# Weights' second part by an accumulating DMA instead of a VectorE subtraction, in a two-layer hybrid inference step

## Chip, core and metric

One core of one Trainium2 chip runs the whole program. The metric is the device time of one execution in microseconds, as the median of several executions.

## What is computed

Two layers of a hybrid backbone, for 512 latent and 128 context tokens of width 2048, in float32. The reference, cut to its trunk:

```python
for l in range(DEPTH):
    hp = _rmsnorm(xp, norm_g[l]) * (1.0 + sc_p) + sh_p
    hs = _rmsnorm(xs, norm_g[l]) * (1.0 + sc_s) + sh_s
    if l % 2 == 0:      # attention and Hyena, one projection in, one out
        out_p, (k_ctx, v_ctx) = _even_mixer(hp, *ev)
        out_s, _ = _even_mixer(hs, *ev, ctx_k=cache_k[:, j], ctx_v=cache_v[:, j])
    else:               # RG-LRU behind a short convolution, times a gate
        out_p, st = _odd_mixer(hp, *od)
        out_s, _ = _odd_mixer(hs, *od, h0=jnp.moveaxis(state_lru[:, j], 1, 0))
    xp = xp + g_p * out_p
    xs = xs + g_s * out_s
```

Each mixer projects all 640 tokens with a large weight matrix (`h @ w_in`, `mixed @ w_out`). The scale, shift and gate vectors come from a second large product, `silu(c) @ mod_w`.

## The kernel before

**The projections.** TensorE multiplies in a rounded float32 (`F32R`), so that each factor is split in two: `wh` is the weight rounded, `wl` what the rounding left, and likewise `h` and `l` for the activations (`mh`, `ml` or `md` for the mixers' outputs). Each product is three matmuls, `wh*h`, `wh*l` and `wl*h`. Weights come in 241 half chunks of 128 x 8 x 128 elements (512 KB). `project` (L810) walks a chunk's two halves over 16 tiles of activations and two column blocks of 320 tokens: 48 matmuls for each half chunk.

**The weight stream.** Class `Stream` (L453) holds three buffers each of `raw`, `wh` and `wl`. `load` (L466) issues the DMA of a half chunk from SyncE's queue. `advance` (L474) rounds it on ScalarE (`wh`) and hands the rest to `finish` (L494), which subtracts on VectorE and then issues the load that takes this half chunk's place in `raw`:

```python
(self.G if self.pooled and i % 2 else self.V).tensor_sub(wl, raw, wh.bitcast(F32))
self.load(i + 1 + RAWS)
```

`pooled` is never set, so all subtractions are VectorE's. `keep_ahead` (L513) splits up to two half chunks ahead of the one that TensorE is using.

**The stages.** A start stage (normalisation, Hyena filters, the first gates; 19 half chunks are split there), attention over eight query chunks q0 to q7 (`attend` L1746, `queries` L1846), Hyena in four blocks of long convolutions (`long_conv` L1958), the first output projection (`out_project` L2224, which also writes `x1d` and scales the tiles `xo` for layer 1), the RG-LRU (`scans` L2367) and the second output projection. In every stage the projections' matmuls (tile `acc`) fill TensorE between the mixers' own work.

**Side sums.** `side_mods` (L661) makes 16 groups of the second product on the side: `mod_w` tiles come by SyncE (`mraw`), ScalarE multiplies (`mprod`) and GpSimd adds up (`macc`), or VectorE does both in one instruction where it is free (from Hyena to the first output projection). A group ends with two small steps on TensorE (`m<-macc,ones`, then `m<-ident,mprod`). The last four tiles of layer 1's input wait for groups 11 and 12 of these.

**The order.** The program is a list of coroutines that a planner (`Order`, `Clock`) runs ahead of time with costs of its own; what it emits is a fixed order on each engine and queue. So a change in one cost or one instruction moves others. An engine runs its order strictly; one that waits holds back everything behind it. The same goes for SyncE, which issues all loads and stores (weights, `mraw`, `ga<-gad` gates, `mixd` and `x1d` stores).

Of the kernel before, what the change touches and what calls it, by code (L numbers as in the profile page):

```python
# [10 lines left out]
F32 = mybir.dt.float32  # L11
F32R = mybir.dt.float32r
AF = mybir.ActivationFunctionType
ALU = mybir.AluOpType
# [160 lines left out]
class Clock:  # L175
# [17 lines left out]
    def __init__(self):  # L193
        self.t = {"PE": 0.0, "V": 0.0, "S": 0.0, "G": 0.0, "Q": 0.0, "DMA": 0.0}
        self.table, self.last = None, 0.0
        self.writes, self.reads, self.start = {}, {}, {}
        self.held = {"V": [], "G": []}
# [255 lines left out]
class Stream:  # L453


    def __init__(self, engines, clock, pool, ahead=2):
        self.V, self.S, self.G, self.Q = engines
        self.pooled = False
        self.clock, self.pool, self.ahead = clock, pool, ahead
        self.src, self.raw, self.parts, self.left = [], {}, {}, {}  # L460
        self.loaded = self.split = self.taken = 0
# [32 lines left out]
    def finish(self, i):  # L494

        if i not in self.left:
            return
        raw, (wh, wl) = self.left.pop(i), self.parts[i]
        (self.G if self.pooled and i % 2 else self.V).tensor_sub(wl, raw, wh.bitcast(F32))
        self.load(i + 1 + RAWS)  # L500

    def take(self, od):
# [20 lines left out]
@with_exitstack  # L523
def tile_kernel(ctx: ExitStack, tc: tile.TileContext, A: dict, O: dict):
    with tc.manual_schedule():
        _kernel(ctx, tc, A, O)


def _kernel(ctx, tc, A, O):
# [6 lines left out]
    def pool_of(stack, name, bufs=1, **kw):  # L536
        return Pool(stack.enter_context(tc.tile_pool(name=name, bufs=bufs, **kw)), clock, bufs)
# [10 lines left out]
    ws = Stream((V, S, G, Q), clock, wpool)  # L548
# [112 lines left out]
    def side_mods(groups, raws, accs, prods, ring):  # L661
        todo = [(l, g, k) for l, g in groups for k in range(16)]
        raw, n = {}, 0
        for j, (l, g, k) in enumerate(todo):
# [17 lines left out]
            for v in range(2):  # L682
                c, a = csil[:, k, v:v + 1], acc[v]
                while True:
                    if clock.t["V"] + IDLE[0] <= od.time and not left[v] and clock.ready([a], [a], "V") <= od.time:
                        if k == 0:
# [933 lines left out]
            V.tensor_scalar(fr[:, :, i, :], yv[:, :, i, :], sc, None, op0=ALU.mult)  # L1620

    IDLE = [99]
    mods = ctx.enter_context(ExitStack())
    mp = pool_of(mods, "mods", bufs=1)
    r_raw = Ring(mp, [128, 512], F32, "mraw", 2)
# [261 lines left out]
    first_out = []  # L1887
    IDLE[0] = 0.5
    with ExitStack() as st:
# [332 lines left out]


    def out_project(op, layer, src, parts, first, keep, finish, xout, sqa, last=None):  # L2224

        r_x = Ring(op, [128, T], F32, "xr", 3 if last else 2)
# [9 lines left out]
        def out(i, x, o):  # L2236
# [10 lines left out]
            def then():  # L2247
                r_x.free(x)
                if keep is not None:
                    Q.dma_start(out=keep[i], in_=o[:, 0:T])  # L2250
                if i == 0:
                    S.activation(sqa, o[:, 0:T], AF.Square)
                else:
                    while not r_sq.ready():
                        yield 0.3
                    sq = r_sq.get()
                    S.activation(sq, o[:, 0:T], AF.Square)
                    yield
                    V.tensor_add(sqa, sqa, sq)
                    r_sq.free(sq)  # L2260
                yield
                yield from finish(i, o)
                yield
                xout[i] = o
# [20 lines left out]
    first_lru = []  # L2285
    IDLE[0] = 0.3
    with ExitStack() as st:
# [38 lines left out]
    parts2, first_out, mixed_done = [None] * 16, [], {}  # L2326
    IDLE[0] = 99
    with ExitStack() as st:
# [447 lines left out]
```

## Time and profile before

| | |
|---|---|
| median of three runs | 2297.33 us (2296.53 to 2302.62) |
| the profiled execution | 2299.91 us, its span 2298.1 us |
| TensorE (PE) busy | 2130.1 us, 93% |
| VectorE (DVE) busy | 1673.0 us, 73% |
| ScalarE (ACT) busy | 1086.3 us, 47% |
| GpSimd (POOL) busy | 845.3 us, 37% |
| DMA | 320.62 MB, 16 engines busy 41.5% |

How to read the rows below. Nearly all instructions are recorded at one line, L318, a helper; they are told apart by tiles, output before the arrow. PE is the matmul, PEld the weight load beside it, SPq SyncE's queue. A window's row gives for PE, PEld, DVE, ACT and POOL the busy time with the number of instructions, then the granted clock of TensorE as a share of full speed, the busy share of the DMA engines and GB/s. A row of waits is: who waited, for whom, us in total, times, the longest. A timeline row is: start, duration, engine, operation, and in brackets the idle time before and what ended it. A row of a group ends with busy time, mean ns of one, and after the bar the engine's idle time before them and what ended most of it. A row of DMA issues ends with KB each and the median us from issue to landing. Matmuls are pipelined, so one lasts 310 ns while the next starts 147 ns after it.

### The profile page before, as it was taken

The numbers are of one execution on the slowest core, as the hardware profiler recorded it, in microseconds if no ns is written. First come the engines' busy times: TensorE is split into PE (matmuls) and PEld (weight loads), VectorE is DVE, ScalarE is ACT, GpSimd is POOL, SyncE is SP. The second block draws the span as 40 slices with busy tenths as digits, with TensorE's granted clock in tenths as the row PEclk, the third lists the DMA queues.
The fourth block names the chain that finished last, engine by engine and source line by source line (L and its number), as shares of the span: only waits on it lengthen the run. The fifth ranks groups of instructions, "written<-read, shape, count | busy, mean of one in ns | idle before, by whom it ended". The sixth has DMA issues, their size and how long they took to land. (4 is left out here: it accounts for less than half of the span.)

```text
span 2298.1 us, 37534 instructions
## 1 busy us (share of the span) xinstructions
PE 2130.1 (93%) x14567; PEld 2025.0 (88%) x14567; DVE 1673.0 (73%) x2560; ACT 1086.3 (47%) x1814; POOL 845.3 (37%) x678
## 2 busy tenths in 40 slices
PE   4899989988989999999998999899999999999997
PEld 1579888877878999999987999799999999999997
DVE  6968775898877888887887676787886667783334
ACT  5555555555553333333353333576565554662222
POOL 3424443445344666566563222444530101110002
PEclk9899999999999999999998999999999999999998
DMA  9864434222225444444455555333322222243223
GB/s 367 301 247 131 136 114 135 84 100 86 93 95 194 140 147 147 140 139 146 148 200 175 191 188 183 98 116 114 117 79 88 85 85 86 80 171 109 97 97 131
DMA packets 127449, 320.62 MB, mean 140 GB/s; under 512 B 14246, under 2 KB 22279, under 8 KB 127272
## 3 DMA queue, kind: packets, MB, share of 16 engines
q1 hardware_dynamic: 125480, 313.20, 40.5%
q0 software_dynamic: 1792, 5.04, 0.7%
q8 instruction: 114, 1.87, 0.3%
q14 instruction: 63, 0.52, 0.1%
HBM read 281.86 MB, written 36.32 MB: 138 GB/s over the span
## 5 line engine op out<-in xcount | busy, mean ns | idle before, releaser
L318 PE MATMUL acc<-h,wh 128*128 128x320 f32 x2544 | 810.0, 318 | 24.9 <-DVE xo L318 9.0
L318 PE MATMUL acc<-h,wl 128*128 128x320 f32 x2544 | 793.0, 312 | 0.0
L318 PE MATMUL acc<-l,wh 128*128 128x320 f32 x2544 | 792.4, 311 | 0.0
L318 POOL TENSOR_TENSOR macc<-macc,mprod 128x512 f32<-128x512 f32 x289 | 434.7, 1504 | 559.2 <-ACT mprod L318 474.1
L318 PEld LDWEIGHTS acc<-h,wh 128*128 128x128 f32 x2544 | 485.2, 191 | 36.0 <-DVE xo L318 9.3
L318 PEld LDWEIGHTS acc<-l,wh 128*128 128x128 f32 x2544 | 484.7, 191 | 0.1
L318 PEld LDWEIGHTS acc<-h,wl 128*128 128x128 f32 x2544 | 483.6, 190 | 0.0
L318 ACT CAST wh<-raw 128x1024 fp32r<-128x1024 f32 x241 | 252.4, 1047 | 413.0 <-PE acc L318 370.0
L318 DVE TENSOR_TENSOR wl<-raw,wh 128x1024 fp32r<-128x1024 f32 x241 | 318.0, 1320 | 171.5 <-ACT wh L318 169.2
L318 PE MATMUL acc<-mh,wh 128*128 128x320 f32 (+2 forms) x1024 | 318.9, 311 | 11.2 <-ACT mh L318 8.8
L318 ACT ACTIVATE mprod<-mraw,vec 128x512 f32<-128x512 f32 x289 | 209.1, 724 | 237.6 <-POOL macc L318 169.5
L318 PE MATMUL acc<-mh,wl 128*128 128x320 f32 (+2 forms) x1024 | 318.3, 311 | 0.0
L318 PE MATMUL acc<-ml,wh 128*128 128x320 f32 (+2 forms) x928 | 288.0, 310 | 2.4 <-DVE ml L318 2.4
L318 DVE SCALAR_TENSOR_TENSOR macc<-mraw,vec,macc 128x512 f32<-128x512 f32 x191 | 186.2, 991 | 100.8 <-DMA mraw<-in_mod_w_dram 77.3
L318 PEld LDWEIGHTS acc<-mh,wh 128*128 128x128 f32 x1024 | 193.2, 189 | 14.6 <-ACT mh L318 9.2
L318 PEld LDWEIGHTS acc<-mh,wl 128*128 128x128 f32 x1024 | 193.6, 189 | 0.0
L318 PEld LDWEIGHTS acc<-ml,wh 128*128 128x128 f32 x928 | 175.1, 189 | 4.1 <-DVE ml L318 3.7
L318 POOL COPY stout<-hs 128x1 f32<-128x1 f32 x32 | 20.5, 639 | 319.2 <-DVE hs L318 319.2
L318 PE MATMUL g<-xhl,wh 128*128 128x322 f32 x512 | 115.7, 314 | 2.2 <-ACT ri L318 2.2
L318 POOL TENSOR_TENSOR y<-y,t 128x256 f32<-128x256 f32 x80 | 84.2, 1072 | 43.0 <-DVE t L318 34.1
L318 POOL TENSOR_TENSOR xo<-xo,sq 128x384 f32<-128x384 f32 (+1 forms) x13 | 11.5, 916 | 239.8 <-ACT sq L318 239.8
L318 DVE SCALAR_TENSOR_TENSOR xo<-acc,modc,xr 128x128 f32<-128x128 f32 (+3 forms) x96 | 38.8, 434 | 82.6 <-PE acc L318 73.7
(303 smaller groups left out, 3369.4 us busy)
## 6 DMA issues: line engine op xcount, KB each, us to landing
mraw<-in_mod_w_dram SPq DMA_DIRECT2D x256, 256.0 KB, 3.3
raw<-in_w_in_dram SPq DMA_DIRECT2D x95, 512.0 KB, 4.0
mraw<-in_mod_w_dram SPq DMA_DIRECT2D x64, 512.0 KB, 7.4
raw<-in_c_in_dram SPq DMA_DIRECT2D x64, 512.0 KB, 3.7
raw<-in_c_out_dram SPq DMA_DIRECT2D x34, 512.0 KB, 3.9
raw<-in_w_out_dram SPq DMA_DIRECT2D x32, 512.0 KB, 4.0
hd<-ef SPq DMA_DIRECT2D x48, 256.0 KB, 3.9
raw<-in_c_gates_dram SPq DMA_DIRECT2D x16, 512.0 KB, 3.5
```

The costliest lines, as they stand in the source:

```text
L318: f(*args, **kw)
```

## The change

From attention on, ScalarE writes the negated `wh` into `wl`, and GpSimd issues a DMA that adds `raw` onto it. VectorE no longer takes part. The start stage keeps the subtraction.

```diff
@@ class Stream, __init__
-        self.pooled = False
+        self.adding = False
@@ class Stream, finish
         raw, (wh, wl) = self.left.pop(i), self.parts[i]
-        (self.G if self.pooled and i % 2 else self.V).tensor_sub(wl, raw, wh.bitcast(F32))
+        if self.adding:
+            self.S.activation(wl, wh.bitcast(F32), AF.Identity, scale=-1.0)
+            self.G.dma_start(out=wl, in_=raw, accum_op=ALU.add)
+        else:
+            self.V.tensor_sub(wl, raw, wh.bitcast(F32))
         self.load(i + 1 + RAWS)
@@ _kernel, after the start stage
     IDLE = [99]
+    ws.adding = True
     mods = ctx.enter_context(ExitStack())
```

Of the 241 half chunks 222 are changed: VectorE has 222 subtractions less, ScalarE 222 negations more, GpSimd 222 DMA issues more. The planner also shares the side sums out anew: 310 instead of 289 products on ScalarE with as many adds on GpSimd, 180 instead of 196 steps on VectorE. TensorE's instructions are the same in number, and so are SyncE's.

Place 1, SyncE at the end of attention (`gad_128` and `gad_129` are the stored gates of q4 and q5, `mixd_84` to `mixd_91` the stored outputs of q0 to q7). Before:

```order
L318 DMA mraw<-in_mod_w_dram 128x512 x3
L318 DMA raw<-in_w_in_dram 128x1024
L318 DMA mixd_90<-mix 128x640
L318 DMA ga<-gad_129 128x640
L318 DMA mixd_89<-mix 128x640
L318 DMA mraw<-in_mod_w_dram 128x512 x3
L318 DMA raw<-in_w_in_dram 128x1024
L318 DMA mraw<-in_mod_w_dram 128x512
L318 DMA mixd_91<-mix 128x640
```

After:

```order
L318 DMA mixd_90<-mix 128x640
L318 DMA ga<-gad_128 128x640
L318 DMA mraw<-in_mod_w_dram 128x512
L318 DMA raw<-in_w_in_dram 128x1024
L318 DMA mixd_88<-mix 128x640
L318 DMA mraw<-in_mod_w_dram 128x512
L318 DMA raw<-in_w_in_dram 128x1024
L318 DMA mraw<-in_mod_w_dram 128x512 x7
L318 DMA mixd_91<-mix 128x640
```

The gate of q4 is now loaded after that of q5 and so late that q4's output is stored third from the end; q7, which needs that buffer, ends seven `mraw` loads behind the last weight load instead of one.

The same place on TensorE, the end of q7 (`sc` scores, `tp` transposes, `o` outputs). Before:

```order
L318 MATMUL o<-pts,vt 64x128 x6
L318 MATMUL tp<-ident,pr 128x128
L318 MATMUL acc<-h_1553,wh 128x320
L318 MATMUL acc<-l_1581,wh 128x320
L318 MATMUL acc<-h_1553,wl 128x320
L318 MATMUL acc<-h_1573,wh 128x320
L318 MATMUL acc<-l_1616,wh 128x320
L318 MATMUL acc<-h_1573,wl 128x320
L318 MATMUL acc<-h_1591,wh 128x320
L318 MATMUL acc<-l_1635,wh 128x320
L318 MATMUL acc<-h_1591,wl 128x320
L318 MATMUL o<-pts,vt 64x128 x2
```

After:

```order
L318 MATMUL tp<-ident,pr 128x128 x8
L318 MATMUL sc<-kh_3809,qhl 128x256
L318 MATMUL sc<-kl_3811,qhl 128x256
L318 MATMUL sc<-kh_3810,qhl 128x256
L318 MATMUL sc<-kl_3812,qhl 128x256
L318 MATMUL o<-pts,vt 64x128 x8
L318 MATMUL tp<-ident,pr 128x128 x7
L318 MATMUL o<-pts,vt 64x128 x6
L318 MATMUL tp<-ident,pr 128x128
L318 MATMUL o<-pts,vt 64x128 x2
L318 MATMUL m<-macc,ones 32x256 x4
L318 MATMUL acc<-h_520,wh 128x320
```

All five blocks of q7 now stand behind the last projection matmul of the attention stage, with no `acc` between them; before, `acc` rows stood between them.

Place 2, TensorE at the end of Hyena, around the last product of the last long convolution (`m<-pinv,y`). Before:

```order
L318 MATMUL io_12531<-invo_7524,yhl 128x256
L318 MATMUL m<-pinv,y 128x128 x4
L318 MATMUL acc<-h_1573,wh 128x320
L318 MATMUL acc<-l_1616,wh 128x320
L318 MATMUL acc<-h_1573,wl 128x320
```

After:

```order
L318 MATMUL acc<-mh_12760,wh 128x320
L318 MATMUL acc<-ml_12671,wh 128x320
L318 MATMUL acc<-mh_12760,wl 128x320
L318 MATMUL m<-pinv,y 128x128 x4
L318 MATMUL acc<-mh_12779,wh 128x320
```

The product now stands in the middle of the output projection (`mh`), no longer in Hyena's last input projection. Between it and the first matmul on the last mixer tiles (`md`) there are 52 `acc` matmuls instead of 100.

The same place on VectorE, between the two halves of the last long convolution (`y<-io`) and the last `md`. Before:

```order
L318 SCALAR_TENSOR_TENSOR g<-g,acc 128x320
L318 TENSOR_TENSOR wl<-raw,wh 128x1024
L318 SCALAR_TENSOR_TENSOR y<-io_12530,frn,t_12838 128x2x128 x2
...
L318 TENSOR_TENSOR ml_12881<-ml_12881,mh_12924 128x640
L318 TENSOR_TENSOR wl<-raw,wh 128x1024
L318 TENSOR_TENSOR md_13008<-o,mh_13009 128x640
L318 SCALAR_TENSOR_TENSOR macc<-mraw,vec,macc 128x512 x2
L318 SCALAR_TENSOR_TENSOR y<-io_12531,frn,t_13017 128x2x128 x2
```

After:

```order
L318 SCALAR_TENSOR_TENSOR g<-g,acc 128x320
L318 TENSOR_TENSOR ml_12767<-ml_12767,mh_12888 128x640
L318 SCALAR_TENSOR_TENSOR y<-io_12561,frn,t_12891 128x2x128 x2
...
L318 TENSOR_TENSOR ml_12773<-ml_12773,mh_12928 128x640
L318 SCALAR_TENSOR_TENSOR macc<-mraw,vec,macc 128x512
L318 TENSOR_TENSOR md_12967<-o,mh_12968 128x640
L318 TENSOR_TENSOR ml_12846<-ml_12846,mh_12973 128x640
L318 TENSOR_TENSOR ml_12848<-ml_12848,mh_12977 128x640
L318 SCALAR_TENSOR_TENSOR y<-io_12562,frn,t_12981 128x2x128 x2
```

Two subtractions and one of two side sums are gone from between the product and the second `y`.

Place 3, TensorE in the first projection of layer 1, where the last four activation tiles (12 to 15) are taken. Before, the last block of these, then a side group:

```order
L318 MATMUL acc<-l_15372,wh 128x322
L318 MATMUL acc<-h_15371,wl 128x322
L318 MATMUL m<-macc,ones 32x256 x4
L318 MATMUL acc<-h_15462,wh 128x322
L318 MATMUL acc<-l_15463,wh 128x322
L318 MATMUL acc<-h_15462,wl 128x322
L318 MATMUL m<-ident,mprod 128x128 x2
L318 MATMUL m<-ones,sqa 128x2 x5
```

After (`h_15224` is tile 11, `h_15347` tile 12):

```order
L318 MATMUL acc<-h_15214,wl 128x322
L318 MATMUL m<-macc,ones 32x256 x4
L318 MATMUL acc<-h_15224,wh 128x322
L318 MATMUL acc<-l_15225,wh 128x322
L318 MATMUL acc<-h_15224,wl 128x322
L318 MATMUL m<-ident,mprod 128x128 x2
L318 MATMUL acc<-h_15347,wh 128x320
L318 MATMUL acc<-l_15348,wh 128x320
```

Before, the side group there was the fourteenth, and the twelfth stood 16 half chunks further up. Now the group there is the twelfth, for which tiles 12 to 15 wait, and it ends directly ahead of tile 12.

## Rows read from the trace of the kernel before

**Rows 1.** The page's first part: busy time, share, instructions of each engine.
```profile
PE 2130.1 (93%) x14567; PEld 2025.0 (88%) x14567; DVE 1673.0 (73%) x2560; ACT 1086.3 (47%) x1814; POOL 845.3 (37%) x678
```

**Rows 2.** Windows: attention, Hyena, first output projection.
```profile
355.00:700.00 345.00, 313.99 (x2299) 283.81 (x2299) 276.05 (x588) 187.38 (x418) 160.20 (x116) 0.99 0.32 104
700.00:1225.00 525.00, 491.24 (x3420) 478.45 (x3419) 428.41 (x536) 197.03 (x327) 321.14 (x251) 0.97 0.47 154
1225.00:1455.00 230.00, 217.94 (x1478) 213.68 (x1476) 160.52 (x192) 91.55 (x145) 58.07 (x34) 1.00 0.55 182
```

**Rows 3.** Waits of TensorE from 355 us on, the longest in total.
```profile
PE tz L318 <- DVE y L318: 12.4, 9, 2.6
PE acc L318 <- DVE xo L318: 11.4, 4, 9.0
PE sc L318 <- ACT pr L318: 9.8, 10, 1.7
PE acc L318 <- ACT mh L318: 8.8, 1, 8.8
PE tp L318 <- ACT pts L318: 8.0, 7, 1.8
PE acc L318 <- DVE g L318: 7.3, 2, 6.2
PE acc L318 <- DVE lu L318: 5.6, 2, 2.8
```

**Rows 4.** The subtraction: its group on the page.
```profile
L318 DVE TENSOR_TENSOR wl<-raw,wh 128x1024 fp32r<-128x1024 f32 x241 | 318.0, 1320 | 171.5 <-ACT wh L318 169.2
```

**Rows 5.** Timeline of ScalarE and VectorE in the second output projection.
```profile
2111.46 1.05 ACT L318 CAST wh<-raw 128x1024 fp32r<-128x1024 f32 x1 [6.00 <-PE acc L318]
...
2118.52 1.05 ACT L318 CAST wh<-raw 128x1024 fp32r<-128x1024 f32 x1 [4.50 <-PE acc L318]
2119.59 1.23 DVE L318 TENSOR_TENSOR wl<-raw,wh 128x1024 fp32r<-128x1024 f32 x1 [5.09 <-ACT wh L318]
```

**Rows 6.** DMA issues: the weight load, and a load that GpSimd issues.
```profile
raw<-in_w_in_dram SPq DMA_DIRECT2D x95, 512.0 KB, 4.0
invo<-in_invo_dram POOLq DMA_DIRECT2D x2, 512.0 KB, 10.7
```

**Rows 7.** DMA queues of the page: packets, MB, share of 16 engines.
```profile
q1 hardware_dynamic: 125480, 313.20, 40.5%
```

**Rows 8.** Timeline of GpSimd: two side sums, and the issue of a load.
```profile
657.24 1.27 POOL L318 TENSOR_TENSOR macc<-macc,mprod 128x512 f32<-128x512 f32 x1 [0.83 <-ACT mprod L318]
659.35 1.28 POOL L318 TENSOR_TENSOR macc<-macc,mprod 128x512 f32<-128x512 f32 x1 [0.83 <-ACT mprod L318]
...
693.30 0.59 POOL L318 DMA_DIRECT2D sig<-in_sig_dram  x1 [2.82 <-PE m L318]
```

**Rows 9.** Waits of SyncE's queue: the longest in total.
```profile
SPq L318 <- DVE wl L318: 1167.7, 226, 12.5
```

**Rows 10.** TensorE's groups from 665 to 700 us, the end of attention.
```profile
L318 PE MATMUL o<-pts,vt 128*64 128x128 f32 x48 | 3.5, 281 | 0.0
L318 PE MATMUL tp<-ident,pr 128*128 128x128 f32 x20 | 3.5, 281 | 0.8 <-ACT pts L318 0.7
```

**Rows 11.** Timeline of TensorE and VectorE at the end of Hyena.
```profile
1186.54 1.05 PE L318 MATMUL m<-pinv,y 128*128 128x128 f32 x8
...
1216.76 0.63 PE L318 MATMUL acc<-mh,wh 128*128 128x320 f32 x1 [8.80 <-ACT mh L318]
...
1191.64 1.40 DVE L318 TENSOR_TENSOR wl<-raw,wh 128x1024 fp32r<-128x1024 f32 x1 [0.44 <-ACT wh L318]
...
1203.75 2.30 DVE L318 TENSOR_TENSOR wl<-raw,wh 128x1024 fp32r<-128x1024 f32 x1
...
1206.92 2.54 DVE L318 SCALAR_TENSOR_TENSOR macc<-mraw,vec,macc 128x512 f32<-128x512 f32 x2
1209.39 0.86 DVE L318 SCALAR_TENSOR_TENSOR y<-io,frn,t 128x256 f32<-128x256 f32 x2
```

## Prediction

> **What bounds the kernel now.** I read the page's first part first: TensorE is busy for 93% of the span, VectorE for 73%, ScalarE for 47%, GpSimd for 37% [rows 1]. The change adds nothing to TensorE and removes nothing from it, so it can only move TensorE's idle time. The windows show where that is: 31 of 345 us in attention, 34 of 525 in Hyena, 12 of 230 in the first output projection [rows 2]. Then the waits say what ends it. From 355 us on VectorE ends 12.4 us (`y`), 7.3 (`g`) and 5.6 (`lu`), together 25.3; ScalarE ends 9.8 (`pr`) and 8.0 (`pts`), together 17.8; one wait for `xo` takes 9.0 and one for `mh` 8.8 [rows 3]. No wait on `wl` is among the long ones: in the steady projection the subtraction is hidden. So the question has three parts: does `wl` stay in time, what do the freed and the newly loaded engines do to those waits, and what does the new order do at its three places.
>
> **The change part by part.**
>
> *Is `wl` in time?* ScalarE rounds one half chunk every 7.06 us (2111.46 to 2118.52), which is TensorE's time for 48 matmuls, so one starts every 0.147 us [rows 5]. The rounding starts when TensorE begins the half chunk two before it, 14.1 us ahead of use. Then follow 1.05 us of rounding, the negation, which I take at the same 1.05 since it has the same size and engine, and the landing of the add. No row shows an accumulating DMA. The nearest are a plain load of the same 512 KB, 4.0 us to landing, and a load of 512 KB that GpSimd issued, 10.7 us, behind three other loads in the same burst [rows 6]. With 4.0 and one more pass of the engines (1.56, below) 5.6: the chain takes 7.7 us and 6.4 are left. With 10.7 it takes 12.8, and 1.3 are left. Both ends fit: 0 us in the steady stretches.
>
> *Do the DMA engines have room?* SyncE's queue moved 313.20 MB in 40.5% of 2298.1 us, 931 us, which makes 337 bytes per ns; 524,288 bytes are 1.56 us of all engines [rows 7]. If the add must read both operands it takes about two passes, 3.12 us for each 7.06 us. The stage with the least room is the first output projection, at a share of 0.55 [rows 2]: 3.88 us of each 7.06. With two passes 7.00 of 7.06, with one 5.44. The new order puts fewer `mraw` loads there (1.6 for each half chunk where there were 2.1, of half a pass each), so I take 6.6, or 94%. Such a stage has bursts that run late. I take +5 us over it; ends 0 (one pass) and +50 (three passes, rival C). Attention at 0.32 and Hyena at 0.47 keep room [rows 2].
>
> The Trainium skill, "Collectives: The Full Stack", section "The bandwidth ceiling: the fold count and why AG ≠ RS ≠ AR", says that an add in the DMA path is slower because it needs two source reads, and that the add itself costs nothing. The trace of before holds no such add, so nothing there confirms it; by that rule the stage fills to 94%, while by a plain copy's count it would stand at some 70% and the term of +5 would be 0.
>
> *VectorE's relief.* 222 subtractions at 1.32 us are 293 us less [rows 4], of 1673. With them go 169 us in which VectorE stood idle before a subtraction until ScalarE's rounding came, with all its later work behind it. It counts only where TensorE waits for VectorE: the 25.3 us of `y`, `g` and `lu`. Ends: 0, if each of those waits is the latency of a chain that no subtraction stands in, and −25.3. These chains run through `acc`, `tz` and ScalarE too, and the subtractions are a sixth of VectorE's work, so a third of it: −8.
>
> *ScalarE's load.* In attention about 26 negations of 1.05 us, 27 us, come on top of 187.38, 15% more [rows 2, 5]. Where one stands ahead of a `pr` or `pts`, TensorE waits longer: 15% of 17.8 is +2.7, less what the idle stretches between take; +2, ends 0 and +18 (each of the 17 waits behind one negation).
>
> *GpSimd's issues.* 222 at 0.59 us are 131 us [rows 8], beside 845 busy of 2298: hidden in idle time, 0. But each issue waits for ScalarE's negation, and the side sums queue behind it.
>
> *SyncE.* Each load of a half chunk into `raw` now waits for the add to land instead of the subtraction, some 5.6 us later instead of 1.2. SyncE already waits there for 1167.7 us over 226 times, 5.2 each [rows 9]. A load takes 4.0 to land and has still a whole period in hand: 0 for the weights. What queues behind it (`mraw`, the `ga` gates, stores) comes later by up to 4.4 us each time; this is what slows the side sums and shapes the three places.
>
> *Place 1, the end of attention.* q7 now stands wholly behind the last projection matmul, with nothing beside it. GpSimd has fourteen side sums in one block behind the last add there, at 2.11 us each (657.24 to 659.35) [rows 8], 29.5 us, and TensorE's next matmul (`m<-macc`) needs them. Two of them can run beside the last projection matmuls; 25 us are left. q7's own matmuls fill 12 of them: 30 `tp` at 0.18, 30 `o` at 0.07 [rows 10], 28 `sc` at about 0.17, scaled by columns from 0.147. That leaves 13 us idle. Before, `pr` and `pts` ended 17.8 us over eight chunks, 2.2 for each [rows 3], so 10.8 are new. The matmuls that stood beside q7 now fill gaps of q5 and q6; I give back their 4.4. So +6; ends 0 (all comes back) and +16 (the gates come late too, and nothing comes back).
>
> *Place 2, the end of Hyena.* Before, the last product ends by 1187.6, and TensorE stands for 8.80 us until 1216.76 for what is made of it. VectorE had a backlog between: among it two subtractions, 0.44 + 1.40 and 2.30 us, and two side sums of 2.54 ahead of the second `y` [rows 11]. The change takes out 4.1 us of subtractions and 1.3 of side sums, and with the product later by 48 matmuls takes away 7.06 of cover: 7.06 − 5.4 = +2; ends −3 (the backlog goes altogether) and +7 (the chain is bound by GpSimd and ScalarE).
>
> *Place 3, the first projection of layer 1.* Tiles 12 to 15 need the twelfth side group, which now ends three matmuls ahead of tile 12. Between lie a copy, a transpose, `modc`, the scaling and the split, about five steps of 1 us, as 0.86 to 1.40 for steps of such sizes show [rows 5, 11], and this chain can hit only the wait; there was one wait of 9.0 us on `xo` in that projection before [rows 3]. +6; ends 0 (this is absorbed by that wait) and +15 (SyncE's `mraw` loads come late as well).
>
> **Sum**: +5 −8 +2 +6 +2 +6 = +13 us on the profiled 2299.91, 2312.9. The median of the runs is 2.58 lower, so 2310.3.
>
> **The rivals.** About 0.3%, 7 us, is what a measurement of this kernel can tell from no change.
>
> *A, faster.* VectorE is what the mixers wait for. The 25.3 us vanish, place 2 gives 3, places 1 and 3 and the DMA engines cost nothing: −28, about 2269; half of it with small costs, about 2283. For it speak the 169 us behind late roundings [rows 4] and the backlog at place 2 [rows 11]; against it that the three places lose cover in the order itself. It decides if places 1 and 3 together cost under what VectorE gives.
>
> *B, no change.* Relief and costs cancel: VectorE gives 15 and the rest costs 15, 2290.4 to 2304.2. TensorE's work is the same and the steady stretches hide both versions.
>
> *C, the DMA engines become the bound.* The point is where an add takes over 3.2 us of all engines in the first output projection (7.06 − 3.88). At three passes, 4.7 us, a half chunk takes 8.6 instead of 7.06, and the 32 half chunks of that stage cost 1.5 each: +50, about 2360 with the other terms. For it speaks the share of 0.55 and that no row shows the add's price; against it that two passes just fit.
>
> That the add doesn't do its work, or that it lands in pieces seen too early, is excluded as a way to a shorter time: TensorE waits for its landing in any case.
>
> **How the numbers follow.** Forecast, slower at 2304 to 2335: 0.43. A 0.20, B 0.23, C 0.14. So faster by over 0.3% is 0.20, within 0.3% 0.23, slower 0.57. The range from 2284 to 2344 leaves out half of A and most of C; the likeliest case's own range is 2304 to 2335.
>
> **What the profile of the changed kernel would show.** VectorE some 290 us less busy, ScalarE some 230 more. An add of 5 to 6 us to landing; over 11.5 would make TensorE wait on `wl` in every period and prove the steady term wrong. In the first output projection a DMA share of about 0.9; at 1.0 with waits on `wl`, C. At the end of attention a stretch of 10 to 15 us with TensorE idle, ended by `macc`, `pr` or `pts`; without it the term of place 1 is wrong. A wait on tile 12's `h` behind the twelfth group. `y`, `g` and `lu` at about 17 us; near 0 would be A.

## The result, and the profile after

The changed kernel takes 2446.78 us (median of four runs, 2444.69 to 2453.41) against 2296.93: a ratio of 1.0652, 95% interval 1.0625 to 1.0679. That is 136 us above the forecast of 2310 and 103 above the upper end of its range, 2344. All times below are medians; every comparison run had the kernel before beside it on the same chip, at 2302, so a difference between the result (before: 2297) and another run is good to some 5 us.

The page's first part of the changed kernel (compare [rows 1]):

```profile
PE 2184.8 (89%) x14567; PEld 2063.9 (84%) x14567; DVE 1412.1 (58%) x2322; ACT 1304.1 (53%) x2052; POOL 984.5 (40%) x921
```

VectorE lost 261 us of work and ScalarE took on 218, near the 290 and 230 of the forecast. TensorE has the same 14567 matmuls but is busy 54.7 us longer, in a span that is 145.6 longer: 55 us of the loss are matmuls at a lower clock, the other 91 are idle time. Its mean granted clock fell from 0.976 to 0.953. The windows show where (attention, Hyena, first output projection; columns as in [rows 2]):

```profile
355.00:745.00 390.00, 339.73 (x2366) 304.69 (x2365) 254.94 (x568) 218.38 (x450) 175.72 (x145) 0.95 0.50 135
745.00:1262.00 517.00, 470.49 (x3222) 457.12 (x3221) 319.14 (x451) 208.23 (x321) 266.58 (x258) 0.96 0.68 187
1262.00:1540.00 278.00, 236.25 (x1500) 228.93 (x1499) 99.38 (x152) 105.92 (x150) 67.95 (x64) 0.91 0.74 198
```

In the first output projection TensorE stands idle for 42 of 278 us at a mean clock of 0.91; before it was 12 of 230 at 1.00. VectorE is busy for 99 of these 278 us and ScalarE for 106: no engine is full. The DMA engines stand at 0.74 on average, so rival C (the engines saturated) did not happen. The queues of the page and the add among the DMA issues (columns as in [rows 7] and [rows 6]):

```profile
q1 hardware_dynamic: 125480, 313.20, 39.0%
q0 software_dynamic: 33760, 121.44, 25.6%
```

```profile
wl<-raw POOLq DMA_DIRECT2D x222, 512.0 KB, 5.3
raw<-in_w_in_dram SPq DMA_DIRECT2D x95, 512.0 KB, 4.2
```

The add takes (25.6% of 2443.7 less the 16 us of the other loads) / 222 = 2.74 us of all engines and lands after 5.3, close to the 3.12 and 5.6 of the prediction. Of TensorE's waits from 355 us on, those for `wl` make 2.8 us in all:

```profile
PE m L318 <- DVE macc L318: 21.4, 3, 9.9
PE sc L318 <- ACT pr L318: 18.3, 16, 4.2
PE acc L318 <- DVE xo L318: 17.3, 5, 6.2
PE io L318 <- POOL y L318: 16.7, 5, 5.6
PE acc L318 <- DVE g L318: 13.3, 6, 3.4
PE tp L318 <- ACT pts L318: 12.5, 8, 2.8
...
PE tz L318 <- DVE y L318: 11.4, 8, 2.6
...
PE acc L318 <- DMA wl<-raw: 2.8, 3, 2.1
```

So the weights' second part is in time, and yet everything is later: `macc`, `xo`, `pr` and `y` (compare [rows 3]). The waits of SyncE's queue, of ScalarE and of VectorE show what stands behind this:

```profile
SPq L318 <- DMA wl<-raw: 1538.4, 218, 17.0
...
ACT mprod L318 <- DMA mraw<-in_mod_w_dram: 226.9, 60, 10.5
...
DVE macc L318 <- DMA mraw<-in_mod_w_dram: 232.2, 58, 12.1
```

Before, SyncE stood 1167.7 us for `wl` [rows 9], and ScalarE and VectorE stood as follows for `mraw`, the side sums' weights:

```profile
DVE macc L318 <- DMA mraw<-in_mod_w_dram: 77.3, 40, 5.2
...
ACT mprod L318 <- DMA mraw<-in_mod_w_dram: 63.0, 33, 5.5
```

These two waits grew from 140 to 459 us. One chain from the timeline, in the first output projection, shows how such a wait gets to TensorE; the columns are as in [rows 5], and the rows are put together engine by engine:

```profile
1406.91 0.88 POOL L318 DMA_DIRECT2D wl<-raw  x1 [1.44 <-ACT wl L318]
...
1406.22 0.38 SPq L318 DMA_DIRECT2D x1d<-xo  x1
1415.08 0.33 SPq L318 DMA_DIRECT2D raw<-in_w_out_dram  x1
1415.51 0.85 SPq L318 DMA_DIRECT2D mraw<-in_mod_w_dram  x2
...
1421.72 0.72 ACT L318 ACTIVATE mprod<-mraw,vec 128x512 f32<-128x512 f32 x1 [5.89 <-DMA mraw<-in_mod_w_dram]
...
1421.73 0.75 DVE L318 SCALAR_TENSOR_TENSOR macc<-mraw,vec,macc 128x512 f32<-128x512 f32 x1 [8.62 <-DMA mraw<-in_mod_w_dram]
1422.39 1.13 DVE L318 SCALAR_TENSOR_TENSOR xo<-acc,modc,xr 128x320 f32<-128x320 f32 x3
...
1422.99 0.63 PE L318 MATMUL acc<-mh,wh 128*128 128x320 f32 x1 [6.20 <-DVE xo L318]
```

GpSimd issues an add at 1406.91. The next load of `raw` takes its source buffer, so SyncE holds that load until the add has landed, here after 8.1 us, and issues it at 1415.08, 8.5 us after its last issue ended. Behind it stands an `mraw` load that needs nothing of this. VectorE has stood 8.62 us before its side sum, with `xo` behind it, and `xo` is what frees an accumulator: TensorE stands 6.20 us. Its next matmul lasts 0.63 us instead of 0.31.

Where the 145 us lie, by the times at which TensorE begins half chunks 20, 45, 95, 127, 180, 205 and 215 (sixteen matmuls on `wl` for each, counted in the trace; the stretches are about those of attention, Hyena, the first output projection and three parts of layer 1):

```
us between half chunks          20-45  45-95 95-127 127-180 180-205 205-215
before                          327.6  483.8  255.2  412.4   181.1    72.2
changed                         361.6  521.3  290.8  420.7   188.9    93.1
new order, subtraction          346.2  482.2  244.3  423.1   191.4    85.9
old order, add                  367.9  578.2  367.1  439.5   183.2    85.7
changed, loads later            326.9  487.3  249.7  408.6   179.4    77.2
subtraction, load before        327.0  504.2  264.2  378.8   181.6    71.8
  the rounding
```

The first two rows are the two kernels; the others are runs of the next section.

### The profile page after: what moved, and what is told of

Read it like the earlier page. It is cut to its first block, busy times and chain, and to the rows that moved or that the text cites. A ratio compares the mean times of both kernels' runs of the same rounds, so it can differ in the third digit from the quotient of the medians.

```text
span 2443.7 us, 38100 instructions
## 1 busy us (share of the span) xinstructions
PE 2184.8 (89%) x14567; PEld 2063.9 (84%) x14567; DVE 1412.1 (58%) x2322; ACT 1304.1 (53%) x2052; POOL 984.5 (40%) x921
## 3 DMA queue, kind: packets, MB, share of 16 engines
q0 software_dynamic: 33760, 121.44, 25.6%
## 5 line engine op out<-in xcount | busy, mean ns | idle before, releaser
L318 POOL TENSOR_TENSOR macc<-macc,mprod 128x512 f32<-128x512 f32 x310 | 449.8, 1451 | 348.4 <-ACT mprod L318 316.4
L318 POOL DMA_DIRECT2D wl<-raw x222 | 195.4, 880 | 766.3 <-ACT wl L318 681.6
L318 ACT ACTIVATE mprod<-mraw,vec 128x512 f32<-128x512 f32 x310 | 223.6, 721 | 395.9 <-DMA mraw<-in_mod_w_dram 226.9
L318 PE MATMUL acc<-mh,wh 128*128 128x320 f32 (+2 forms) x1024 | 327.4, 320 | 23.4 <-DVE xo L318 17.3
L318 PE MATMUL acc<-mh,wl 128*128 128x320 f32 (+2 forms) x1024 | 325.3, 318 | 0.7 <-DMA wl<-raw 0.7
L318 PE MATMUL acc<-ml,wh 128*128 128x320 f32 (+2 forms) x928 | 296.5, 320 | 8.8 <-DVE ml L318 8.6
L318 DVE SCALAR_TENSOR_TENSOR macc<-mraw,vec,macc 128x512 f32<-128x512 f32 x170 | 155.5, 936 | 250.1 <-DMA mraw<-in_mod_w_dram 217.4
L318 ACT ACTIVATE wl<-wh 128x1024 fp32r<-128x1024 f32 x222 | 234.2, 1055 | 2.1
L318 PEld LDWEIGHTS acc<-mh,wh 128*128 128x128 f32 x1024 | 200.0, 195 | 28.8 <-DVE xo L318 18.6
L318 PEld LDWEIGHTS g<-xhl,wh 128*128 128x128 f32 x512 | 89.2, 196 | 14.4 <-ACT ri L318 13.8
L318 DVE SCALAR_TENSOR_TENSOR w<-w 128x644 f32<-128x644 f32 x64 | 70.7, 1104 | 42.0 <-ACT w L318 40.8
```

Of the source, the lines that this page charges most:

```text
L318: f(*args, **kw)
```

## The experiments

Theory S says that SyncE's queue is the place: it stands behind each add, and what is queued there comes late. The rivals: O, the new order with its lost cover; A, ScalarE's 222 negations; D, the added traffic of the DMA engines. A fourth had no run of its own: GpSimd, in strict order too, stands for each negation before it issues the add, 681.6 us in all, with its side sums behind. A trick separates the order from the work: the planner fixes the order from the costs it is told, so it can be told of one way of making `wl` while another is emitted. The order of all other instructions stays that of the one, the work is the other's.

**The new order, with the subtraction.**

```diff
-            self.S.activation(wl, wh.bitcast(F32), AF.Identity, scale=-1.0)
-            self.G.dma_start(out=wl, in_=raw, accum_op=ALU.add)
+            self.V.engine.tensor_sub(wl, raw, wh.bitcast(F32))
+            self.clock.note("S", "activation", (wl, wh.bitcast(F32), AF.Identity), {"scale": -1.0})
+            self.clock.note("G", "dma_start", (), {"out": wl, "in_": raw})
```

> The planner is told of the negation and the add, so that every engine keeps the order of the changed kernel, but the work is done by VectorE's subtraction as before. Theory S (SyncE's queue stands until each add has landed, some 4 us longer than for a subtraction, and the side loads, gates and stores behind it come late): most of the 150 us goes, 2300 to 2335. Rival O (the new order itself, which has less cover beside the mixers' chains): 2400 to 2445. Rivals A (ScalarE's 222 negations stand ahead of the mixers' steps) and D (the adds crowd the DMA engines) expect the same as S here.

Measured: 2340.51 us, 1.0173 (1.0155 to 1.0191), just above S's 2335. The order alone costs 38 us, the work in that order 106 more (110 by the ratios). The waits (SyncE, ScalarE, VectorE):

```profile
SPq L318 <- DVE wl L500: 1026.5, 207, 13.7
...
ACT mprod L318 <- DMA mraw<-in_mod_w_dram: 17.5, 12, 3.8
...
DVE macc L318 <- DMA mraw<-in_mod_w_dram: 9.9, 7, 3.7
```

459 us of waits for `mraw` are down to 27. O has its share, 38 of about 145, and no more.

**The old order, with the add** (the reverse of that edit: negation and add are emitted, the planner is told of the subtraction).

> The reverse: the planner is told of the subtraction, so that every engine keeps the order of the kernel before, but the work is done by ScalarE's negation and the DMA's add. S, A and D: 2400 to 2480, as slow as the changed kernel or slower, since nothing is planned for the late landing. O: 2295 to 2330.

Measured: 2594.29 us, 1.1272 (1.1251 to 1.1293), much above what S named as its upper end. In an order that is not planned for it the add costs 292 us:

```profile
SPq L318 <- DMA wl<-raw: 1625.7, 214, 17.3
...
ACT mprod L318 <- DMA mraw<-in_mod_w_dram: 306.5, 70, 10.0
...
DVE macc L318 <- DMA mraw<-in_mod_w_dram: 321.2, 62, 12.3
```

The planner's new order thus costs 38 us with the subtraction and saves some 147 with the add. It spreads the side sums out to half chunk 210, where they ended at 159; that this is what saves them was not tried by itself. As the main cause of the loss O is refuted.

**SyncE's wait without the rest.** The subtraction and the order of before; GpSimd also stores the half chunk to DRAM, in one run from `raw` (shown), in the other from `wh`. Only the first holds back the next load.

```diff
         (self.G if self.pooled and i % 2 else self.V).tensor_sub(wl, raw, wh.bitcast(F32))
+        if self.adding:
+            self.G.engine.dma_start(out=self.spare, in_=raw)
```

> The kernel before, in its order, with the subtraction; behind each of the 222 subtractions GpSimd also stores the half chunk raw to a spare place in DRAM. The next load must then wait for that store to land, some 4 us more, while neither VectorE nor ScalarE has any work less or more and the weights' second part is in time. S: 2360 to 2440, with ScalarE and VectorE waiting for mraw two to three times as long as before (63 and 77 us). A and O: 2297 to 2310. D: the same as the next run.

> As the run before, but the store takes the rounded first part instead of raw, so that no load waits for it; the DMA engines carry the same bytes and GpSimd issues as much. S: 2297 to 2312. D: as slow as the store of raw, 2340 or more. A and O: 2297 to 2310.

Measured: 2425.25 us (1.0539, 1.0521 to 1.0557) with `raw`, 2340.94 (1.0172, 1.0144 to 1.0199) with `wh`. The stores land in 3.5 and 3.2 us, so both carry the same. The waits with the store of `raw`:

```profile
SPq L318 <- DMA spare<-raw: 1001.4, 181, 12.5
...
ACT mprod L318 <- DMA mraw<-in_mod_w_dram: 186.7, 59, 7.8
...
DVE macc L318 <- DMA mraw<-in_mod_w_dram: 179.8, 56, 11.5
```

and with the store of `wh`:

```profile
SPq L318 <- DVE wl L318: 1176.9, 224, 12.5
...
ACT mprod L318 <- DMA mraw<-in_mod_w_dram: 87.9, 43, 6.2
...
DVE macc L318 <- DMA mraw<-in_mod_w_dram: 106.4, 43, 5.2
```

The two are 84 us apart, with `wl` in time and the work of VectorE and ScalarE as before: that is what the wait for the landing is worth here, with one reservation. The stores also hold GpSimd differently: it stands 582.0 us for ScalarE's rounding before the stores of `wh`, and 252.0 for the store before and 146.4 for a weight load before those of `raw`. S had expected the store of `wh` to cost nothing, and it costs 39: the bytes, the 222 issues or GpSimd's standing, and which of them was not tried. Across the four kernels in the old order time follows the waits for `mraw`: 140 us at 2302, 194 at 2341, 366 at 2425, 628 at 2594. From one order to another these waits say less: in the new order with the subtraction 27 us of them stand beside 2341.

**The loads later.** The changed kernel, but each last step loads the half chunk two further on, whose buffer was left an add earlier.

```diff
-        self.load(i + 1 + RAWS)
+        self.load(i + RAWS + (not self.adding))
```

> The changed kernel, but from attention on each half chunk's last step issues the load of the half chunk two further on instead of three, whose buffer the add of the half chunk before has long left. SyncE no longer waits for the add that was just issued. S: SyncE's wait for wl falls from 1538 us below 400, ScalarE's and VectorE's waits for mraw from 227 and 232 us below 100 each, and the time to 2320 to 2370. A (ScalarE's negations) and D (crowded DMA engines): 2420 to 2450.

Measured: 2301.95 us, 1.0007 (0.9993 to 1.0020): the whole loss is gone, 145 us, more than S had given. The adds and negations are all there, as its page shows; the planner shares the side sums out a little differently (the lines below the first are columned as in [rows 4]):

```profile
PE 2140.9 (93%) x14567; PEld 2031.7 (88%) x14567; DVE 1465.1 (64%) x2374; ACT 1271.7 (55%) x2000; POOL 924.0 (40%) x868
...
L318 POOL DMA_DIRECT2D wl<-raw x222 | 195.2, 879 | 842.5 <-ACT wl L318 752.1
...
L318 ACT ACTIVATE wl<-wh 128x1024 fp32r<-128x1024 f32 x222 | 234.3, 1055 | 2.3
```

```profile
SPq L318 <- DMA wl<-raw: 735.1, 154, 15.5
...
ACT mprod L318 <- DMA mraw<-in_mod_w_dram: 32.8, 17, 4.1
...
DVE macc L318 <- DMA mraw<-in_mod_w_dram: 109.0, 46, 8.1
```

SyncE's wait did not fall below 400 as expected but to 735, and VectorE's to 109, not below 100. That suffices: the waits for `mraw` are 142 us together, as in the kernel before with its 140. So the length of SyncE's standing is not what counts (it was 1168 before, at the same time), but whether the loads behind it come late.

The negations and the adds' traffic cost nothing by themselves: they are all there at 2302, and so is GpSimd's standing for the negation, 752.1 us where the changed kernel had 681.6. The first output projection carries the adds in the time that it took before, with more DMA traffic than in the changed kernel (compare [rows 2]):

```profile
1225.00:1455.00 230.00, 221.94 (x1504) 216.81 (x1502) 118.70 (x183) 108.37 (x156) 44.81 (x43) 1.00 0.90 246
```

A and D are thereby refuted as costs that come with the work whatever the loads do. The edit also lets the planner order anew, so part of the 145 is a better order; the next run parts the two.

**The same order, with the subtraction.** The trick of the first run on this kernel.

> The order of the changed kernel with its loads later (2302), but with VectorE's subtraction in place of the negation and the add. If that kernel's add, negation and freed VectorE all together are worth nothing once SyncE doesn't wait (S): 2290 to 2315. If the freed VectorE was worth tens of us there, and covered some cost of the add: 2325 to 2380. If the add still cost as much as VectorE gave: below 2285.

Measured: 2306.41 us, 1.0018 (1.0005 to 1.0031), against 1.0007 for the add in this order. The intervals overlap: freeing VectorE of 222 subtractions, with all that it costs elsewhere, is worth some 3 us of 2300 at best, and perhaps nothing. With the subtraction the new order took 2341 and this one takes 2306, so some 35 of the 145 us come with the new order itself; the other 110 show only with the add.

**The two halves apart.** In the changed kernel's order, ScalarE negates and VectorE adds; or VectorE negates and the DMA adds.

```diff
-            self.G.dma_start(out=wl, in_=raw, accum_op=ALU.add)
+            self.V.engine.tensor_tensor(wl, raw, wl.bitcast(F32), op=ALU.add)
+            self.clock.note("G", "dma_start", (), {"out": wl, "in_": raw})
```

```diff
-            self.S.activation(wl, wh.bitcast(F32), AF.Identity, scale=-1.0)
+            self.V.engine.tensor_scalar(wl, wh.bitcast(F32), -1.0, None, op0=ALU.mult)
+            self.clock.note("S", "activation", (wl, wh.bitcast(F32), AF.Identity), {"scale": -1.0})
```

> The order of the changed kernel, with ScalarE's negation as in the changed kernel, but VectorE adds raw instead of the DMA. ScalarE has its whole new load, no load waits for a DMA's add. S: 2335 to 2360, within 20 us of the run with the new order and the subtraction (2340). A: 2390 to 2445.

> The order of the changed kernel, with the DMA's add as there, but VectorE makes the negation, so that ScalarE has none of its new load. S: 2420 to 2460, as the changed kernel. A: 2340 to 2390.

Measured: 2393.46 us (1.0408, 1.0386 to 1.0430) and 2479.99 (1.0777, 1.0762 to 1.0792). The first lies in A's band, not in S's (2335 to 2360): 53 us above the same order with the subtraction. Its VectorE, in strict order, stands before each add until the negation is made:

```profile
DVE wl L501 <- ACT wl L318: 373.2, 150, 6.4
```

So this run mixes ScalarE's load with a new wait on VectorE: what ScalarE's negations cost in the changed kernel's order stays open, between nothing and 53 us. The second lies above both bands. With ScalarE relieved the kernel gets no faster, it is some 30 us slower than the changed one, which speaks against A; but VectorE has the negations instead, so it is no proof.

**The true price told to the planner.** It had counted 3.5 us to landing; the edit makes it 5.3, and 1.76 passes of the DMA engines.

```diff
-            end = self.t["DMA"] = begin + size / 360e3
+            slow = 1.76 if kw.get("accum_op") is not None else 1.0
+            self.t["DMA"] = begin + size * slow / 360e3
+            end = self.t["DMA"] + (0.7 if slow > 1 else 0.0)
```

> The changed kernel with its loads where they are, but the planner counts the add as long as the trace shows it, 5.3 us to landing instead of 3.5, and 2.6 us of the DMA engines instead of 1.5. If the order is bad because the planner did not know the price: 2300 to 2370. S, by which SyncE waits for the add whatever the order: 2400 to 2460.

Measured: 2432.11 us, 1.0563 (1.0545 to 1.0581). Knowing the price saves 15 to 20 us. SyncE still stands for the add:

```profile
SPq L320 <- DMA wl<-raw: 1516.4, 217, 17.9
```

**The load before the rounding**, with the add, and with the subtraction from attention on or from the first output projection on.

```diff
@@ def advance
-        self.load(i + 1)
+        self.load(i + (RAWS if self.adding else 1))
@@ def finish
-        self.load(i + 1 + RAWS)
+        if not self.adding:
+            self.load(i + 1 + RAWS)
```

> The changed kernel with its add, but the load of the half chunk two further on is issued before a half chunk is rounded (as in the run of the subtraction with the load there). No load stands behind an add that was just issued, and the side sums end at half chunk 133 in this order instead of 209. S: 2270 to 2310, no wait of TensorE above 10 us in total on mixers' steps from layer 1 on. If the add costs by itself (A or D): 2330 or more.

> The kernel before with its subtraction, but from attention on the load of the half chunk two further on is issued before a half chunk is rounded, instead of that three further on after its subtraction. If SyncE's wait behind the newest half chunk, 1088 us from attention on in the kernel before, also costs there, as S would have it by the 140 us that ScalarE and VectorE wait for mraw: 2240 to 2285. If these waits are covered in an order planned with them: 2290 to 2320.

> The kernel before with its subtraction, but the load of the half chunk two further on is issued before the rounding only from the first output projection on; attention and Hyena keep their order. In the run with this from attention on, layer 1 was 34 us shorter, with the side sums ended before it, and Hyena and the first output projection 29 us longer. If the gain comes with the side sums' early end: 2265 to 2290. If it was bought with Hyena's loss: 2295 to 2310.

Measured: 2384.92 us with the add (1.0340, 1.0314 to 1.0366), a clear miss, in the band given to A and D; 2294.30 (0.9971, 0.9960 to 0.9981) and 2293.19 (0.9958, 0.9944 to 0.9973) with the subtraction, the last between its two bands. With the add SyncE still waits, since here the load comes before the rounding and so sooner after the add that it needs:

```profile
SPq L318 <- DMA wl<-raw: 1008.8, 183, 15.7
```

```profile
1250.00:1520.00 270.00, 230.86 (x1429) 219.80 (x1429) 107.06 (x177) 100.32 (x144) 54.88 (x51) 0.91 0.80 215
```

The side sums end early, at half chunk 133, which packs the first output projection (this window): DMA share 0.80, and the waits for `mraw` add up to 385 us. The first part of layer 1 (half chunks 127 to 180) gets 19 us shorter, the stages before it 87 longer and what follows 20 longer. The traffic alone is not the cause, since the kernel with the later loads ran at 0.90 there without loss; whether the waits or the packing of the side sums weigh more was not parted. With the subtraction the early end makes the first part of layer 1 34 us shorter, and Hyena and the first output projection 29 longer. Moving the loads only from the first output projection on kept Hyena at its old time, but gave 23 us in the first part of layer 1 and took 17 in that projection: most of the gain is bought. Still, this version has the lowest median of the study, 0.4% below the kernel before; the interval of the run above it overlaps.

## Why the prediction was wrong, step by step

- *`wl` in time*: right. 5.3 us to landing (5.6 taken), 2.8 us of waits on `wl` in all. *DMA engines*: right in its price, 2.74 us an add against 3.12. The first output projection stood at 0.74 of the engines instead of 0.94, since it got longer; in its old length, in the kernel with the later loads, it stood at 0.90 and cost nothing, so of the +5 nothing showed.
- *VectorE's relief*: taken at −8 of a possible −25. In one order, that of the later loads, `g`, `y` and `lu` hold TensorE for 37.4 us with the subtraction and 20.3 with the add, so the waits themselves gave more than the 8. The time shows only some −3 of it (2302 against 2306), and other waits grew beside it, `yhl` from 5.0 to 10.1 us and `macc` from nothing to 7.6.
- *SyncE*: **this step failed.** "A load takes 4.0 to land and has still a whole period in hand: 0 for the weights" was right. The delay of what queues behind it "by up to 4.4 us each time" named the mechanism, and the sum then priced it only at the three places where the order had changed. In the runs it can cost at any of the 222 half chunks: SyncE stands for an add 218 times, 7.1 us each where it stood 5.2 before, and a stand delays `mraw` loads, on which ScalarE and VectorE wait in strict order, with `xo`, `pr` and `y` behind them. In the old order 84 us lie between a store that holds back the load and one that doesn't; letting the load take another buffer's turn gives all 145 back, some 35 of it by the order. The term should have been some 100 us. SyncE's 1167.7 us of waiting [rows 9] were read as slack for all that the queue carries, and they were it only for the weights; the rows that bear on the rest, the 140 us that ScalarE and VectorE already waited for `mraw`, do not enter it.
- *ScalarE's load*: of the +2 nothing showed in the order of the later loads, where `pr` and `pts` hold TensorE for 13.4 us without the negations and 12.2 with them. What it cost in the changed kernel's order is not known.
- *The three places*: +14 in sum; the new order with the old work costs 38. By stages, attention (place 1) is 18.6 us longer in that run, Hyena 1.6 and the first output projection (place 2) 10.9 shorter, the first part of layer 1 (place 3) 10.7 longer, and 24.0 are lost behind half chunk 180, where no place was named and where the side sums now go on to half chunk 210. At the end of attention q7 did stand uncovered in the changed kernel:

```profile
705.71 0.66 PE L318 MATMUL tp<-ident,pr 128*128 128x128 f32 x4 [1.02 <-ACT pts L318]
707.51 0.39 PE L318 MATMUL sc<-kh,qhl 128*128 128x256 f32 x1 [1.14 <-ACT pr L318]
713.62 0.90 PE L318 MATMUL tp<-ident,pr 128*128 128x128 f32 x3 [3.54 <-DVE sm L318]
715.18 0.48 PE L318 MATMUL tp<-ident,pr 128*128 128x128 f32 x1 [0.65 <-DVE pts L318]
724.40 0.42 PE L318 MATMUL acc<-h,wh 128*128 128x320 f32 x1 [2.62 <-ACT ub L318]
...
1571.24 0.63 PE L318 MATMUL acc<-h,wh 128*128 128x320 f32 x1 [7.68 <-ACT h L318]
```

  The first four add up to 6.4 us, near the +6 of the sum but by luck, since `macc` is not among them: q7's own chain sets the time, not the fourteen side sums; soon after, a matmul of Hyena's input projection waits 2.62 for ScalarE. At place 2 the wait of 8.80 us for `mh` [rows 11] and one of 2.47 for `md` are gone, and the longest there are now 2.74 for `ml` and 2.50 for `mprod`: some 6 us gained where +2 was taken. At place 3 the wait behind the twelfth side group came as forecast, the last row above with its 7.68 us, but the wait of 9.0 for `xo` [rows 3] just ahead of it is gone: about −1 where +6 was taken, near the end "this is absorbed by that wait".
- *Rivals*: none of the three was this. C had the size nearest to it and the wrong place: not the engines' room but the queue that waits for a landing.

## What to carry to other kernels

When a short engine step is replaced by a DMA, ask which queue must now wait for its landing before it can reuse the source buffer, and list everything that queue issues behind that wait. A queue that shows long waits is not idle: they are slack only if nothing urgent stands behind them in order, and that shows in the waits of the engines that the queue feeds, not in its own. If a buffer's release gets later, try to let the queue ask for it one turn later; and to part an order's cost from its work's, keep the one fixed while changing the other.

## What the runs showed of the hardware

An accumulating DMA of 512 KB onto an on-chip tile takes 2.74 us of all sixteen engines, 1.76 times the 1.56 of a load of as many bytes, and lands 5.3 us after its issue begins, of which GpSimd is busy 0.88 (the plain issue of [rows 8] took 0.59). It lands later where the engines are fuller: after 4.6 us in the window of attention (DMA share 0.50) and 5.8 in that of the first output projection (0.74), as medians in the changed kernel. The Trainium skill, "Collectives: The Full Stack", section "The bandwidth ceiling: the fold count and why AG ≠ RS ≠ AR", puts the add of a reduce-scatter at two source reads; the trace agrees nearly, at 1.76 passes.

Idle time costs twice. After the stand of 6.20 us before 1422.99 TensorE's granted clock is 0.50 of full speed, that is its level of 1.2 GHz (columns as in [rows 2]):

```profile
1423.00:1426.00 3.00, 3.00 (x11) 3.00 (x12) 1.28 (x3) 2.18 (x3) 2.07 (x2) 0.50 0.14 26
```

The first matmul there lasts 0.63 us and the next ones 0.47, against 0.31 at 1.00 (2.4 GHz) before the stand. Of the 145.6 us that the span grew, 54.7 are the same matmuls taking longer.
